# A decoder layer on one core: key-tile rotation on another engine, a third plain column block, a later split of the first down chunk

## The chip, the cores and the metric

One core of one Trainium2 chip runs the whole kernel. The metric is the device time of one execution in microseconds. Engines carry the profile's names: PE is TensorE (matmuls; PEld its weight loads), DVE is VectorE, ACT is ScalarE, POOL is GpSimd, SP is SyncE, which here only issues DMAs.

## What is computed

One layer of a decoder on 512 tokens of width 1024, all in float32, with three residual blocks:

```python
y = hybrid_mixer(rms_norm(x, pre_mix_g), w_in, attn_gn_g, ret_gn_g, w_out)
x = x + rms_norm(y, post_mix_g)
y = memory_cross_attn(rms_norm(x, pre_mem_g), mem, mem_norm_g, w_q_mem, w_kv_mem, w_o_mem)
x = x + rms_norm(y, post_mem_g)
y = (silu(g) * u) @ w_down          # g, u = split(rms_norm(x, pre_ffn_g) @ w_gate_up), hidden width 2816
x = x + rms_norm(y, post_ffn_g)
```

The mixer projects the input to queries, keys and values of 8 attention heads (64 wide) and of 4 retention heads (128 wide). Attention queries and keys get a rotary turn of their first 16 dimensions: `t * cos + swapped(t) * sin`. That turn of the keys is one place of the change; the SwiGLU at the end is the other.

## The kernel before

**Precision.** A float32 product is made of three passes of a faster type: every operand is split into a high part `h` (a cast, on ACT) and a low part `l` (the rest, a subtraction, on DVE; `split`, lines 90 and 91), and `mm3` (lines 84 to 86) adds up h*h, h*l and l*h in one PSUM bank. There are 8 PSUM banks of 128x512 (`bank`), 20 SBUF units of 128x2048 (`unit`, of which a split operand, `pair`, takes two), and 2 buffers for raw weights (`raw`).

**Order.** The program is traced in the order in which it is written. At build time the framework puts each engine's instructions in a fixed order, from the written order and its own estimate of when inputs are ready; a buffer goes to a new tile once the last reader of the old one is through. On the chip every engine works through its own queue in order. Inside `tc.manual_schedule()` (the loop over `step`) the written order is kept.

**Attention projections.** `head_proj` makes four tiles of two heads each for queries (`aq`) and then for keys (`ak`), f = 0 to 3: 24 matmuls of 128x512 each into one bank. Then DVE writes `t1 = ps * cos` (line 457) and `t2 = shuffle(ps)` (line 458); a multiply by sin (460) and an add (461) follow, on POOL for f = 0 to 2 and on DVE for f = 3. `flush` then splits the tile before: for keys `split_k` casts two halves on ACT (430), subtracts on DVE (432), copies on ACT (433), and moves the low half to the other 64 partitions by a DMA from POOL's queue (434). `att_scores` (lines 492 and 493) multiplies queries by these keys; its second matmul reads what that DMA wrote. Three banks hold one head's scores until DVE has masked them (497). The written order at the end of the keys is: ak 1, ak 2, scores of head 0, ak 3, scores of head 1, then the four value tiles `av`, each in one bank. At this time the last retention head is being normalised as well: its small DVE chain (186 to 190), its scaling on ACT (407) and its product with the gate on POOL (410).

**SwiGLU.** There are 22 column blocks of 128 gate and 128 up columns. A block is computed in one of two ways. `plain(f, j, n, ps)` is the direct product: for gate or up (j), for token half n, 24 matmuls of 128x256 (2 input halves, 4 chunks, 3 passes); a block has four such calls, 96 matmuls, and keeps two banks (`pg`). `step(f)` gets the same from seven block products in place of eight, 84 matmuls of 128x256, and needs sums of the weight blocks (`blocks_sum`), their split (`blocks_b`) and sums of the transposed input (T1 to T4). In a step, `ffn_c1` copies product 1 to `s1` (ACT, line 929), `ffn_c11` adds product 2 (DVE, 933), later adds read the other products (979, 981, 983, 984, 937). Product 7 goes into the bank that line 933 reads, product 3 into the one that line 979 reads.

Weights of a block come by one DMA into `raw` (`blocks_fetch`); `blocks_a` casts them on ACT (131), writes the negated cast (134), and a DMA from POOL's queue adds the weights onto that (135), which leaves the low part `wal`. For a plain block this is 2048 columns in pieces of 512, for a step 1536 in pieces of 768.

Two blocks (`PRE = 2`) are plain. They run while the last two token blocks of the layer before, `hb` and `hc`, are normalised and transposed (`to_b`, line 868, into B12 and B22 and the sums T): first both blocks for token half 0, then both for half 1. The operands of steps 2 and 3 are prepared in between. Then come steps 2 to 21. A step issues the loads, sums and splits of blocks after it, ahead of its own line 933. In the last step (f = 21) there is no block after it, and in that place stands `load()`, which splits the first chunk of the down weights (lines 90 and 91, two pieces).

**Down projection.** `down` multiplies the activations by `w_dn`: 11 chunks of 48 matmuls of 128x512, into all 8 banks. `split_a` reads the activations back from DRAM and splits them, the low part on POOL (1045).

Of the kernel before, what the change touches and what calls it, by code (L numbers as in the profile page):

```python
# [38 lines left out]
def hybrid_layer(ctx, tc, t, out):  # L39
    nc = tc.nc  # L40
# [9 lines left out]
    def uname(p):  # L50
        cnt[0] += 1
        return f"{p}{cnt[0]}"

    def bank(name):
        return psp.tile([P, 512], F32, tag="ps", name=uname(name))

    def unit(name, dt=F32):
        return up.tile([P, 2048], dt, tag="u", name=uname(name))

    def pair(name):  # L60
        return unit(name + "h", F32R), unit(name + "l", F32R)

    def work(name):
        return wk.tile([P, 512], F32, tag="w2k", name=uname(name))
# [14 lines left out]
    def part(pr, c0, n):  # L79
        return pr[0][:, c0:c0 + n], pr[1][:, c0:c0 + n]  # L80

    def mm3(o, sta, mov, start, stop):
        (sh, sl), (mh, ml) = sta, mov
        nc.tensor.matmul(o, lhsT=sh, rhs=mh, start=start, stop=False)  # L84
        nc.tensor.matmul(o, lhsT=sh, rhs=ml, start=False, stop=False)  # L85
        nc.tensor.matmul(o, lhsT=sl, rhs=mh, start=False, stop=stop)  # L86

    def split(src, hi, lo, scale=None):
        if scale is None:
            nc.scalar.copy(hi, src)  # L90
            nc.vector.tensor_sub(lo, src, hi.bitcast(F32))  # L91
        else:
            nc.scalar.mul(hi, src, scale)
            nc.vector.scalar_tensor_tensor(lo, src, scale, hi.bitcast(F32), op0=ALU.mult, op1=ALU.subtract)
# [6 lines left out]
    def fetch(key):  # L101
        fetched[key] = raw = rawp.tile([P, 2048], F32, tag="raw", name=uname("raw"))
        nc.sync.dma_start(raw, t[key[0]][key[1]])
# [6 lines left out]
    def blocks_fetch(f):  # L110
        chunks.remove(("w_gu", f))
        raws[f] = rawp.tile([P, 2048], F32, tag="raw", name=uname("raw"))
        nc.sync.dma_start(raws[f], t["w_gu"][f])

    def blocks_sum(f, names):
        if f not in sums:
            sums[f] = unit("sums")
        a11, a12, a22, a21 = (raws[f][:, i * 512:(i + 1) * 512] for i in range(4))
        s2, s4, s1, s3 = (sums[f][:, i * 512:(i + 1) * 512] for i in range(4))
        for name in names:  # L120
            e = nc.gpsimd if name in ('s3', 's4') else nc.vector
            if name == "s1":
                e.tensor_add(s1, a21, a22)
            else:
                e.tensor_sub(*{"s2": (s2, s1, a11), "s3": (s3, a11, a21), "s4": (s4, a12, s2)}[name])  # L125

    def blocks_a(f, n=1536, m=768):
        w = was[f] = pair("wa")
        for c0 in range(0, n, m):
            c = slice(c0, c0 + m)  # L130
            nc.scalar.copy(w[0][:, c], raws[f][:, c])  # L131
        for c0 in range(0, n, m):
            c = slice(c0, c0 + m)
            nc.scalar.mul(w[1][:, c], w[0][:, c].bitcast(F32), -1.0)  # L134
        nc.gpsimd.dma_start(w[1][:, :n], t["w_gu"][f][:, :n], accum_op=ALU.add)  # L135

    def blocks_b(f, i):
        if f not in wbs:
            wbs[f] = pair("wb")
        split(sums[f][:, i * 1024:(i + 1) * 1024], *part(wbs[f], i * 1024, 1024))  # L140
# [22 lines left out]
    def take(name, i, ahead=2):  # L163
        while (name, i) not in loaded:
            load()
        while chunks and len(loaded) - 1 < ahead:
            load()
        return loaded.pop((name, i))
# [61 lines left out]
    def hx(k, c0, n):  # L230
        return part(hT[k // 4], (k % 4) * S + c0, n)
# [209 lines left out]
    def flush():  # L441
        while late:
            fn, f, v = late.pop()
            fn(f, v)

    def head_proj(c0, store, name):
        ws = {}

        def one(f):
            if f % 2 == 0:  # L450
                ws[0] = take("w_in", c0 + f // 2)
            w = ws[0]
            ps = bank(name)
            for k in range(KT):
                mm3(ps, part(w, k * 256 + (f % 2) * P, P), hx(k, 0, S), k == 0, k == KT - 1)
            t1, t2 = work("t1"), work("t2")
            nc.vector.tensor_mul(t1, ps, rope[:, 2, :])
            nc.vector.stream_shuffle(t2, ps, swap)
            e = nc.vector if f == 3 else nc.gpsimd
            e.tensor_mul(t2, t2, rope[:, 3, :])  # L460
            e.tensor_add(t1, t1, t2)
            flush()
            late.append((store, f, t1))

        return [lambda f=f: one(f) for f in range(4)]
# [137 lines left out]
    ak = head_proj(10, split_k, "ak")  # L603
# [308 lines left out]
    def product(i, w, ps):  # L912
        u, c0, name = prods[i]
        for k in range(4):
            x_ = bx[name][:, k * H:(k + 1) * H], bx[name][:, 1024 + k * H:1024 + (k + 1) * H]
            mm3(ps, part(w[u], c0 + k * P, P), x_, k == 0, k == 3)
# [3 lines left out]
    def ffn_p12(f):  # L920

        w, p = (was[f], wbs[f]), bank("p")
        product(1, w, p[:, :H])
        product(2, w, p[:, H:])
        ffn[f] = w, p, work("s1"), work("c"), work("u")

    def ffn_c1(f):
        w, p, s1, c, u = ffn[f]
        nc.scalar.copy(s1[:, :H], p[:, :H])

    def ffn_c11(f):
        w, p, s1, c, u = ffn[f]
        nc.vector.tensor_add(c[:, :H], s1[:, :H], p[:, H:])

    def ffn_done(f):
        w, p, s1, c, u, r = ffn[f]
        nc.vector.tensor_add(c[:, H:], c[:, H:], r[:, H:])  # L937
        nc.scalar.activation(c, c, AF.Silu)  # L938

    def keep(f, v):  # L940
        nc.sync.dma_start(ad[:, f * S:(f + 1) * S], v)

    def ffn_mult(f):
        c, u = ffn.pop(f)[3:5]
        nc.vector.tensor_mul(c, c, u)
        keep(f, c)

    def step(f):
        nxt = f + 1 < FT
        two = f + 2 < FT  # L950
        ffn_p12(f)
        w, p, s1, c, u = ffn[f]
        if f + 3 < FT:
            blocks_fetch(f + 3)
        else:
            fetch(("w_dn", f + 3 - FT))
        if f > PRE:
            ffn_done(f - 1)
        if two:
            blocks_sum(f + 2, ("s3", "s1", "s2"))  # L960
        ffn_c1(f)
        if f > PRE:
            ffn_mult(f - 1)
        if nxt:
            blocks_b(f + 1, 1)
        else:
            load()
        ffn_c11(f)
        q, r = bank("q2"), bank("r")
        ffn[f] += (r,)  # L970
        product(4, w, q[:, :H])
        product(6, w, r[:, :H])
        if two:
            blocks_sum(f + 2, ("s4",))
        if nxt:
            blocks_b(f + 1, 0)
        if two:
            blocks_a(f + 2)
        nc.vector.tensor_add(s1[:, H:], s1[:, :H], r[:, :H])
        product(5, w, q[:, H:])  # L980
        nc.vector.tensor_add(c[:, H:], s1[:, H:], q[:, H:])
        product(7, w, p[:, :H])
        nc.vector.tensor_add(s1[:, :H], s1[:, H:], p[:, :H])
        nc.vector.tensor_add(u.rearrange("p (i s) -> p i s", i=2), q.rearrange("p (i s) -> p i s", i=2),
                             s1[:, None, :H].to_broadcast([P, 2, H]))
        product(3, w, r[:, H:])
        for d in (raws, was, sums, wbs):
            d.pop(f, None)


    PRE = 2

    def plain(f, j, n, ps):
        for i, (c0, name) in enumerate(((0, "B1%d"), (512, "B2%d")) if j == 0 else ((1536, "B1%d"), (1024, "B2%d"))):
# [4 lines left out]

    pg = {f: (bank("g"), bank("u")) for f in range(PRE)}  # L1000
    for f in range(PRE):
        blocks_fetch(f)
        blocks_a(f, 2048, 512)
    blocks_fetch(2)
    for f in range(PRE):
        for j in range(2):
            plain(f, j, 0, pg[f][j])
        if f == 0:
            late_splits = [to_b(hb, 2, nc.gpsimd)]
    late_splits.append(to_b(hc, 3))  # L1010
    blocks_a(2)
    blocks_sum(2, ("s3", "s1", "s2", "s4"))
    blocks_fetch(3)
    for f in range(PRE):
        for j in range(2):
            plain(f, j, 1, pg[f][j])
        if f == 0:
            for e in late_splits:
                e()
            late_splits.clear()  # L1020
        del was[f], raws[f]
        sg = work("sg")
        nc.scalar.activation(sg, pg[f][0], AF.Silu)
        nc.vector.tensor_mul(sg, sg, pg[f][1])
        keep(f, sg)
        blocks_b(2, 1 - f)
    pg.clear()
    del bx["B12"]
    blocks_a(3)
    blocks_sum(3, ("s3", "s1", "s2", "s4"))  # L1030
    blocks_fetch(4)
    xd = tc.dram_tile([S, D], F32, name="xd")
    for b in range(TB):
        nc.sync.dma_start(xd[b * P:(b + 1) * P, :], x[b])
# [150 lines left out]
```

## Time and profile before

| | |
|---|---|
| median of 3 runs | 802.81 us (799.59 to 955.97) |
| the profiled execution | 801.05 us |
| its span, first to last instruction | 799.3 us |
| outside the span | 1.75 us |
[...]
| busy, of the span | PE 98%, PEld 87%, DVE 63%, ACT 48%, POOL 25% |

Times in the rows are microseconds from the start of the span. A row of the timeline gives the start, the busy time, engine, line and operation, output and inputs, how many instructions are merged in it and, in brackets, how long the engine sat idle before it and who released it. PE's matmuls are pipelined: the busy time of one matmul overlaps the next one's, so that two matmuls of 256 columns start about 0.12 us apart while each is shown with 0.28 us, and two of 512 columns 0.23 us apart while each has 0.39.

### The profile page before, as it was taken

The page shows a single profiled execution, that of the slowest core. Times are in us where ns is not written, and L with a number is a line of the kernel's source. Part 1 is how long each engine was busy: PE and PEld are TensorE (multiplying, and loading weights), DVE is VectorE, ACT ScalarE, POOL GpSimd, SP SyncE. Part 2 cuts the span into 40 slices and gives each one's busy share as a digit, 9 for nine tenths or more (in the row PEclk, how much of TensorE's full clock was granted, in tenths as well). Part 3 has the DMA queues.
Part 4 walks back from the last instruction along what each step waited for, and adds up shares of the span by engine and source line. Part 5 has one row for each costly group of instructions (what it writes and reads, how often), then busy time and mean ns, then how long its engine had stood idle before and what let it go on. Part 6 is the DMA issues. An engine that isn't in the chain of part 4 may idle for free.

```text
span 799.3 us, 12220 instructions
## 1 busy us (share of the span) xinstructions
PE 780.2 (98%) x4828; PEld 695.8 (87%) x4828; DVE 502.5 (63%) x1002; ACT 386.4 (48%) x667; POOL 201.1 (25%) x177
## 2 busy tenths in 40 slices
PE   9999999899999999999999989999999999999996
PEld 7788888777887888999988989999999998888885
DVE  6497368574666657757567797667777767541143
ACT  6522424485563824445437575555555545542011
POOL 0163033420111100400000654333333326551000
PEclk9999999989999999999999999999999999999999
DMA  8634313223135430525008288777777793864011
GB/s 324 268 132 155 109 53 106 66 79 119 54 106 204 170 154 0 182 83 192 19 28 214 80 243 220 208 210 206 208 208 205 208 267 117 310 250 171 1 52 53
DMA packets 24489, 120.60 MB, mean 151 GB/s; under 512 B 2928, under 2 KB 2928, under 8 KB 14960
## 3 DMA queue, kind: packets, MB, share of 16 engines
q1 hardware_dynamic: 19904, 99.89, 34.3%
q0 software_dynamic: 3808, 18.88, 12.6%
q10 hardware_dynamic: 720, 1.06, 0.4%
q8 instruction: 38, 0.62, 0.3%
q14 instruction: 19, 0.16, 0.1%
HBM read 108.80 MB, written 9.96 MB: 149 GB/s over the span
## 4 chain that ended last, share of the span: by engine, by line
PE 52%; DVE 4%; issue 0%; ACT 0%; DVEq 0%; ACTq 0%
PE dn L84 5%; PE dn L85 5%; PE dn L86 5%; PE p L84 3%; PE p L86 3%; PE p L85 3%; PE q L85 3%; PE q L86 3%; PE q L84 3%; PE r L84 2%; PE r L86 2%; PE r L85 2%; PE o L84 2%; PE o L85 2%; PE o L86 2%; DVE wbl L91 1%
## 5 line engine op out<-in xcount | busy, mean ns | idle before, releaser
L91 DVE TENSOR_TENSOR wl<-raw,wh 128x1024 fp32r<-128x1024 f32 (+1 forms) x91 | 120.0, 1354 | 69.1 <-ACT wh L90 39.0
L90 ACT CAST wh<-raw 128x1024 fp32r<-128x1024 f32 (+1 forms) x91 | 90.0, 1038 | 61.4 <-DMA raw<-in_w_in 29.3
L91 DVE TENSOR_TENSOR wbl<-sums,wbh 128x1024 fp32r<-128x1024 f32 x40 | 51.2, 1280 | 30.3 <-ACT wbh L90 30.3
L84 PE MATMUL dn<-wh,ah 128*128 128x512 f32 x176 | 68.5, 389 | 0.0
L85 PE MATMUL dn<-wl,ah 128*128 128x512 f32 x176 | 68.5, 389 | 0.0
L86 PE MATMUL dn<-wh,al 128*128 128x512 f32 x176 | 68.5, 389 | 0.0
L135 POOL DMA_DIRECT2D wal<-in_w_gu x22 | 19.5, 887 | 176.1 <-ACT wal L134 117.5
L1045 POOL TENSOR_TENSOR al<-af,ah 128x512 fp32r<-128x512 f32 x22 | 36.1, 1673 | 43.9 <-ACT ah L1044 43.9
L84 PE MATMUL p<-bB,wah 128*128 128x256 f32 x160 | 45.3, 283 | 0.0
L85 PE MATMUL p<-bB,wah 128*128 128x256 f32 x160 | 45.3, 283 | 0.0
L86 PE MATMUL p<-bB,wal 128*128 128x256 f32 x160 | 45.3, 283 | 0.0
L90 ACT CAST wbh<-sums 128x1024 fp32r<-128x1024 f32 x40 | 40.2, 1051 | 3.4 <-POOL sums L125 1.8
L125 POOL TENSOR_TENSOR sums<-raw,sums 128x512 f32<-128x512 f32 x20 | 34.1, 1705 | 25.4 <-DVE sums L125 25.4
L86 PEld LDWEIGHTS dn<-wh,al 128*128 128x128 f32 x176 | 33.0, 188 | 6.9
L84 PEld LDWEIGHTS dn<-wh,ah 128*128 128x128 f32 x176 | 33.0, 188 | 6.8
L85 PEld LDWEIGHTS dn<-wl,ah 128*128 128x128 f32 x176 | 33.0, 188 | 6.8
L134 ACT ACTIVATE wal<-wah 128x768 fp32r<-128x768 f32 (+1 forms) x48 | 36.6, 809 | 0.0
L85 PE MATMUL q<-hhl,wh 128*128 128x256 f32 x128 | 36.2, 284 | 0.2 <-DVE hhl L91 0.2
L938 ACT ACTIVATE c<-c 128x512 f32<-128x512 f32 x20 | 12.7, 632 | 49.1 <-DVE c L937 49.1
L84 PE MATMUL q<-hhh,wh 128*128 128x256 f32 x128 | 35.8, 284 | 0.3 <-ACT hhh L90 0.3
L86 PE MATMUL q<-hhh,wl 128*128 128x256 f32 x128 | 36.1, 283 | 0.0
L131 ACT CAST wah<-raw 128x768 fp32r<-128x768 f32 (+1 forms) x48 | 35.9, 803 | 0.0
(346 smaller groups left out, 2521.5 us busy)
## 6 DMA issues: line engine op xcount, KB each, us to landing
raw<-in_w_gu SPq DMA_DIRECT2D x22, 1024.0 KB, 4.9
wal<-in_w_gu POOLq DMA_DIRECT2D x20, 768.0 KB, 7.3
raw<-in_w_in SPq DMA_DIRECT2D x12, 1024.0 KB, 5.0
raw<-in_w_dn SPq DMA_DIRECT2D x11, 1024.0 KB, 5.0
raw<-in_w_kv SPq DMA_DIRECT2D x8, 1024.0 KB, 4.7
ad<-c SPq DMA_DIRECT2D x20, 256.0 KB, 4.0
af<-ad SPq DMA_DIRECT2D x5, 1024.0 KB, 7.3
x<-in_x SPq DMA_DIRECT2D x4, 1024.0 KB, 9.5
```

The lines of the kernel that those rows point to most:

```text
L84: nc.tensor.matmul(o, lhsT=sh, rhs=mh, start=start, stop=False)
L85: nc.tensor.matmul(o, lhsT=sh, rhs=ml, start=False, stop=False)
L86: nc.tensor.matmul(o, lhsT=sl, rhs=mh, start=False, stop=stop)
L90: nc.scalar.copy(hi, src)
L91: nc.vector.tensor_sub(lo, src, hi.bitcast(F32))
L125: e.tensor_sub(*{"s2": (s2, s1, a11), "s3": (s3, a11, a21), "s4": (s4, a12, s2)}[name])
L131: nc.scalar.copy(w[0][:, c], raws[f][:, c])
L134: nc.scalar.mul(w[1][:, c], w[0][:, c].bitcast(F32), -1.0)
L135: nc.gpsimd.dma_start(w[1][:, :n], t["w_gu"][f][:, :n], accum_op=ALU.add)
L938: nc.scalar.activation(c, c, AF.Silu)
L1045: nc.gpsimd.tensor_sub(lo[:, c], v[:, c], hi[:, c].bitcast(F32))
```

## The change

The multiply and the add of the rotation go to DVE for all four key tiles; query tiles stay as they were. `PRE` becomes 3: block 2 is computed the plain way, and everything that was prepared for steps 2, 3 and fetched for 4 is now prepared for 3, 4 and fetched for 5. The two halves of `blocks_b` for the first step now follow the second and the third plain block. In the last step `load()` moves behind `ffn_c11`; for the other steps the order stays.

```diff
@@ head_proj
-            e = nc.vector if f == 3 else nc.gpsimd
+            e = nc.vector if f == 3 or name == 'ak' and f in (0, 1, 2) else nc.gpsimd
@@ step
         if nxt:
             blocks_b(f + 1, 1)
-        else:
+        ffn_c11(f)
+        if not nxt:
             load()
-        ffn_c11(f)
@@
-    PRE = 2
+    PRE = 3
@@
     for f in range(PRE):
         blocks_fetch(f)
         blocks_a(f, 2048, 512)
-    blocks_fetch(2)
+    blocks_fetch(PRE)
...
-    blocks_a(2)
-    blocks_sum(2, ("s3", "s1", "s2", "s4"))
-    blocks_fetch(3)
+    blocks_a(PRE)
+    blocks_sum(PRE, ("s3", "s1", "s2", "s4"))
+    blocks_fetch(PRE + 1)
...
-        blocks_b(2, 1 - f)
+        if f:
+            blocks_b(PRE, 2 - f)
...
-    blocks_a(3)
-    blocks_sum(3, ("s3", "s1", "s2", "s4"))
-    blocks_fetch(4)
+    blocks_a(PRE + 1)
+    blocks_sum(PRE + 1, ("s3", "s1", "s2", "s4"))
+    blocks_fetch(PRE + 2)
```

## Rows read from the trace of the kernel before

**Rows 1.** The page, part 1: busy time of each engine over the span.

```profile
PE 780.2 (98%) x4828; PEld 695.8 (87%) x4828; DVE 502.5 (63%) x1002; ACT 386.4 (48%) x667; POOL 201.1 (25%) x177
```

**Rows 2.** Waits of PE: who waited for whom, total, times, longest.

```profile
PE p L84 <- DVE c L933: 3.8, 2, 2.2
PE av L84 <- DVE t L458: 2.9, 1, 2.9
```

**Rows 3.** Busy time by stretch: PE, PEld, DVE, ACT, POOL, clock, DMA share, GB/s.

```profile
161.50:168.00 6.50, 6.45 (x16) 5.13 (x17) 4.64 (x15) 3.69 (x5) 3.64 (x4) 0.54 0.21 42
460.00:480.00 20.00, 17.24 (x140) 16.66 (x139) 19.64 (x24) 14.75 (x21) 10.93 (x8) 1.00 0.85 251
660.00:680.00 20.00, 18.33 (x123) 16.81 (x122) 14.01 (x16) 11.49 (x17) 12.52 (x8) 1.00 0.36 115
680.00:700.00 20.00, 20.00 (x90) 16.58 (x89) 10.30 (x6) 10.14 (x15) 11.14 (x6) 1.00 0.78 299
780.00:800.00 20.00, 12.10 (x54) 9.69 (x52) 7.43 (x21) 3.85 (x9) 0.00 (x0) 0.89 0.14 53
```

**Rows 4.** Timeline of PE around the key tiles.

```profile
150.59 0.47 PE L493 MATMUL s<-kl,qk 128*128 128x512 f32 x1 [1.46 <-DMA kl<-kl]
...
161.55 0.80 PE L84 MATMUL av<-wh,hTh 128*128 128x512 f32 x1 [2.92 <-DVE t L458]
```

**Rows 5.** Timeline of DVE around the key tiles.

```profile
152.67 0.73 DVE L458 STREAM_SHUFFLE t<-ak 128x512 f32<-128x512 f32 x1
158.72 1.41 DVE L432 TENSOR_TENSOR kl<-t,qk 64x512 fp32r<-64x512 f32 x2 [5.32 <-ACT qk L430]
...
160.77 0.72 DVE L458 STREAM_SHUFFLE t<-ak 128x512 f32<-128x512 f32 x1
...
168.25 0.69 DVE L460 TENSOR_TENSOR t<-t,rope 128x512 f32<-128x512 f32 x1
```

**Rows 6.** Timeline of POOL around the key tiles.

```profile
143.36 1.29 POOL L460 TENSOR_TENSOR t<-t,rope 128x512 f32<-128x512 f32 x1 [4.12 <-DVE t L458]
...
154.14 1.28 POOL L410 TENSOR_TENSOR rg<-rz,rg 128x512 f32<-128x512 f32 x1 [1.62 <-ACT rz L407]
...
156.75 1.29 POOL L461 TENSOR_TENSOR t<-t,t 128x512 f32<-128x512 f32 x1
```

**Rows 7.** DVE's rotation of the last query tile.

```profile
137.98 1.81 DVE L461 TENSOR_TENSOR t<-t,t 128x512 f32<-128x512 f32 x1
```

**Rows 8.** POOL's instruction at the same time.

```profile
137.94 1.29 POOL L410 TENSOR_TENSOR rg<-rz,rg 128x512 f32<-128x512 f32 x1 [1.62 <-ACT rz L407]
```

**Rows 9.** Timeline of PE: the first step (f = 2).

```profile
475.15 0.35 PE L84 MATMUL p<-bT,wbh 128*128 128x256 f32 x1 [2.16 <-DVE c L933]
...
477.29 0.39 PE L84 MATMUL r<-bB,wbh 128*128 128x256 f32 x1 [0.47 <-DVE s L979]
```

**Rows 10.** Timeline of DVE: line 933 in steps 3 and 4.

```profile
484.41 0.41 DVE L933 TENSOR_TENSOR c<-s,p 128x256 f32<-128x256 f32 x1
...
494.48 0.41 DVE L933 TENSOR_TENSOR c<-s,p 128x256 f32<-128x256 f32 x1
```

**Rows 11.** Timeline of ACT between the plain products.

```profile
439.94 0.60 ACT L687 ACTIVATE junk<-o 128x512 bf16<-128x512 f32 x1 [3.75 <-PE o L86]
...
444.94 1.06 ACT L196 ACTIVATE junk<-x 128x1024 bf16<-128x1024 f32 x1 [4.31 <-DVE x L699]
```

**Rows 12.** Timeline of PE: transposes of the last token block.

```profile
452.06 1.04 PE L868 MATMUL tp<-ident,h 128*128 128x128 f32 x8
```

**Rows 13.** Tile wal, 415 to 480 us: durations (min/median/max ns), and DMAs.

```profile
L134 ACT ACTIVATE wal<-wah x14: 636/680/850, 422.1 to 476.8; 128x512 fp32r<-128x512 f32 x8, 128x768 fp32r<-128x768 f32 x6
...
DMA to landing us min/median/max: 6.9/7.8/11.4
```

**Rows 14.** Timeline of DVE: the last step (f = 21).

```profile
664.70 4.12 DVE L91 TENSOR_TENSOR wl<-raw,wh 128x1024 fp32r<-128x1024 f32 x2 [0.36 <-ACT wh L90]
```

**Rows 15.** Timeline of PE: the last step.

```profile
669.29 0.35 PE L84 MATMUL p<-bT,wbh 128*128 128x256 f32 x1 [1.67 <-DVE c L933]
```

## The prediction

> **What bounds the kernel now.** I read the page's busy times first. PE is busy 98% of the span, 780.2 of 799.3 us [rows 1], and of the 19 us that it idles, 7 lie in the last stretch, where the final block leaves the chip [rows 3]. So nothing that only relieves another engine can pay, unless PE waits for that engine; and 2% of 802.81 us, 16 us, which is about what a measurement of this kernel can tell from no change, is more than all PE waits in the middle hold together. Next I read the waits of PE. The two largest are a product of the steps that waits for DVE's line 933, twice, 3.8 us, and the first value tile, which waits 2.9 us for DVE's shuffle [rows 2]. The windows show where these sit: in 460 to 480 PE is busy 17.24 of 20 us and DVE 19.64, in 660 to 680 PE 18.33 [rows 3]. [...] The change touches just these three places, so I price them one by one.
>
> A wait in brackets counts from the modelled end of the matmul before. Starts follow each other faster than these ends (0.23 apart at 0.39 us, 0.12 at 0.28), so PE's real loss is 0.16 us more than each idle shown.
>
> **Part 1, the key tiles.** What PE loses: 1.46 + 0.16 = 1.6 us before the second scores matmul, which waits for the DMA of the low key half [rows 4]; 2.92 + 0.16 = 3.1 us before the value tile [rows 4]; and 16 matmuls in 6.45 us where 16 x 0.23 = 3.7 would do, 2.7 us [rows 3]. Together 7.4 us, the upper bound.
>
> Why it waits: DVE shuffles a key tile, POOL takes 1.29 us each for multiply and add [rows 6], and only then may ACT cast and DVE subtract (line 432). DVE's queue is in order, so it stands idle in front of line 432, 5.32 us for key tile 1 [rows 5], and behind line 432 stands the shuffle of key tile 2. That shuffle is the last reader of the bank that the first value tile needs; all other banks hold scores or key tile 3. For tile 1 it was worse than two POOL operations: its shuffle was through at 153.4 [rows 5], POOL first did the gate product at 154.14, and its add ended at 156.75 + 1.29 = 158.0 [rows 6].
>
> With the change DVE itself does the two, 0.69 us each, as tile 3 shows [rows 5], with no hand-over. Six are added, 4.1 us of DVE; they lie in the 2 to 5 us that DVE idles per tile, so I charge them nothing as work, only as delay in the chain. If that cover were gone, 4.1 us of delay would be the price.
> - Tile 0: POOL started at 143.36 and took two times 1.29 [rows 6]; DVE needs 1.4. The DMA is issued 1.2 to 1.5 us earlier. The 1.6 us gap shrinks to about 0.2: gain 1.4 (bounds 0, if DVE first does its statistics for the retention head, and 1.6).
> - Tile 1: the chain ends at 153.4 + 1.4 = 154.8 in place of 158.0, 3.2 us earlier, and what stands ahead of it (a weight split behind tile 0's casts) also moves up by what tile 0 gains. Line 432 and the shuffle of tile 2 follow 3 to 4.6 us earlier. PE wants the bank 1.4 us earlier than its old 158.5. So of the 3.1 us gap 0 to 2.0 are left; I take 0.5: gain 2.6.
> - The clock: idles of 1.46 [rows 4] and 2.16 us [rows 9] left it at full speed (the stretch 460 to 480 shows 1.00 [rows 3]), the one of 2.92 us halved it. With 0.5 left I take the whole 2.7; the bound is 0.
>
> Sum of part 1: 1.4 + 2.6 + 2.7 = 6.7 us; from 1.1 (the gap stays at 2.0 and the clock still falls) to 7.4. POOL loses six operations of 1.29 us, and its only other work here is the key DMAs and the gate product, which come no later. Behind this stage PE stays full, so I take the gain as carried to the end: what feeds it (ACT's casts) was held by the same POOL chain.
>
> One row speaks against the move. DVE's add for the last query tile took 1.81 us [rows 7], where the same add takes 0.69; POOL's gate product ran beside it from 137.94 for 1.29 us [rows 8], and DVE was through 0.56 us behind POOL. [...] The moved pair of tile 1 would meet the gate product of 154.14. By this the gap keeps 1.1 us more (1.81 - 0.69) and the sum below would be 792.4, a time inside the forecast's own range, with some 0.2 of its chance.
>
> **Part 2, the third plain block.** It adds 96 matmuls of 128x256 and drops a step of 84. Lines 933 of two steps lie 494.48 - 484.41 = 10.07 us apart [rows 10], 0.12 us a matmul: 12 x 0.12 = 1.4 us more for PE, with nothing to hide it. A plain block is 96 x 0.12 = 11.5 us.
>
> What it takes away: in the first step PE loses 2.16 + 0.16 and 0.47 + 0.16 = 3.0 us [rows 9], both to DVE, which is full (19.64 of 20 us [rows 3]) with sums and splits that stand in its queue ahead of lines 933 and 979. With 11.5 us more of plain products in front of the first step, and only one more gate product (0.7 us) for DVE, that backlog (late by 2.3 us now) is done 11.5 - 0.7 - 2.3 = 8 us before it is needed. Gain 3.0, net 1.6. What is late next: steps 3 and on, where PE loses nothing.
>
> New in the preamble is the preparation of block 2: eight ACT operations of about 0.68 us [rows 13], 5.4 us, one DMA that lands up to 11.4 us after its issue [rows 13], two more units and two more PSUM banks. Before 440 all 20 units are taken, by my count of live tiles (residual 2, gains 1, w_o 8, cross-attention output 2, raw B 1, B11 and B21 2, two plain weight pairs 4). The first w_o chunk is free 18 matmuls before the output projection ends at 439.9 [rows 11], at 439.9 - 18 x 0.23 = 435.8. ACT idles 3.75 and 4.31 us on either side of 440 [rows 11], so the casts fit there, the DMA goes out at about 442 and lands at 450 to 453. PE reaches the point behind the second block at 452.06 [rows 12]. So the new block may cost PE 0 to 1 us there, and I take 0, as the scores and transposes of hc can go first. Banks: 6 for the plain blocks and 2 for each transposed pair make 8, the pair of hb being copied out before hc's. On SP's queue the fetch of block 4 now waits for the casts of block 2 instead of its sums: earlier, not later. Part 2 ranges from a gain of 2.0 (some short waits for hc's splits close too) to a loss of 7 (rivals).
>
> **Part 3, the last step.** Line 933 stood behind the two splits of the down chunk, 4.12 us from 664.70 [rows 14], and product 7 waited 1.67 + 0.16 = 1.8 us for it [rows 15]. Moved ahead, line 933 goes in the 0.36 us in which DVE waited for ACT's cast [rows 14], and the splits start where they did. Now line 979 is behind them, at 668.8, and ends at 669.2; product 7 then ends at 667.5 + 1.4 = 668.9, so product 3 loses 0.3. Gain 1.5. The splits end no later, so the first down matmul has its weights; the fetch for this chunk was issued two steps before, so no DMA moves.
>
> **The sum.** 6.7 + 1.6 + 1.5 = 9.8 us, made against the profiled execution's 801.05 us (span 799.3 and 1.75 outside it): **791.3 us**. That execution lies 1.8 us under the median, 802.81, and between the two lower runs.
>
> **Rivals.**
> - *Key chain still too slow* (chance 0.16). DVE no longer waits for POOL, but ACT's cast stands in ACT's queue behind the four retention scalings, or DVE's queue puts other work between. For it: every tile crosses DVE and ACT twice. Against: 3 us and more of margin were worked out. Part 1 gives 1.4 + 1.1 and the clock still falls: 801.05 - 2.5 - 1.6 - 1.5 = 795.4 us.
> - *Low part of block 2 late* (0.10). If its casts go only at 440.6, in ACT's second idle time, they end at 446, the DMA at 446.9 + 11.4 = 458.3. If PE's queue has block 2 next, it idles from 452.06, 6.2 us, and at half clock behind that 2.7. Part 2 becomes 6.2 + 2.7 + 1.4 - 3.0 = 7.3 us of loss: 801.05 - 6.7 - 1.5 + 7.3 = 800.2 us. For it: the units are full until 435.8. Against: PE has hc's transposes and half 1 of two blocks to do first.
> - *Slower* (0.07). The casts of block 2 get units that come free late. The residual is written until 444.94 [rows 11] and then copied out by a DMA, 6.9 us at the least by the nearest row [rows 13]: 452. If the casts stand in ACT's queue ahead of line 196 and wait for that unit, line 196 starts at 452 + 5.4 = 457.4 and all of hc is 12.5 us late; PE runs dry after two half blocks. It decides once the unit comes free later than 444.94. Part 2 is then 12.5 + 2.7 + 1.4 - 3.0 = 13.6 us of loss: 801.05 - 6.7 - 1.5 + 13.6 = 806.5 us. For it: 20 of 20 units taken. Against: ten units of the output projection come free first.
> - *Nothing gained* (0.07). The framework orders other instructions anew and gives the gain back: about 801 us. That the edits don't take effect can't be: the engine is named, and the loop keeps the written order.
>
> **How the numbers follow.** The forecast has 0.60. Its own range is 789.9 (all gaps closed: 7.4 + 2.0 + 1.8) to 794. A range of 787.5 to 800.5 takes in the first two rivals, and a run's scatter of some 2 us below. Only the sum of all gaps and some luck could pass 786.8 us: faster by over 2% gets 0.05. Slower by over 2% would be 818.9 us, past every case: 0.03. Within 2%: 0.92.
>
> **What would show it.** Part 1: the bracket at the first value tile under 1 us, the one before the second scores matmul near 0, clock 1.00 in 160 to 180, and no lines 460 and 461 on POOL for key tiles. Part 2: no wait of the first step (now f = 3) for lines 933 and 979, and PE full from 440 on; a gap at about 452 would be the late DMA. Part 3: product 7 of the last step without a wait, product 3 waiting about 0.3 for line 979. The prediction is wrong if PE still idles over 2 us at one place between 140 and 480 with the lower clock behind it, or if its first down matmul, at about 672 now, does not come some 10 us earlier.

## The result and the profile after

| | before | after |
|---|---|---|
| median of 4 runs each | 802.01 us (799.59 to 955.97) | 789.53 us (789.17 to 790.12) |
| the profiled execution | 801.05 us | 789.65 us |
| its span | 799.3 us | 787.9 us |
| granted TensorE clock over the span (1.00 is full speed) | 0.993 | 0.998 |

The ratio is 0.9855, 95% interval 0.9829 to 0.9881: 1.5% faster. The interval is a good deal narrower than the 2% that the prediction held to be about the least one can tell here. One slow execution of the kernel before, 955.97 us, counts in the median of the table and not in the ratio. Between the profiled executions 11.4 us are gone; 9.8 were forecast.

The page after, part 1, answers to [rows 1]: PE is now 99% of the span, with 12 matmuls more and 2.9 us less busy time. The stretch at a granted clock of 0.54 [rows 3], which is gone, had alone cost 2.7 us.

```profile
PE 777.3 (99%) x4840; PEld 694.5 (88%) x4840; DVE 498.3 (63%) x998; ACT 384.9 (49%) x668; POOL 189.1 (24%) x169
```

The waits of PE after, the three largest. Lines 933 and 458 of [rows 2] are gone from this list; of the wait for the key's DMA 0.4 us is left, and the two others stand ahead of 101 us, where nothing was edited.

```profile
PE warm L261 <- POOL ones L242: 1.0, 1, 1.0
PE bc L222 <- DVE diag L221: 0.6, 1, 0.6
PE s L493 <- DMA kl<-kl: 0.4, 1, 0.4
```

Busy time by stretch after, to set beside [rows 3] (columns as there). Where 16 matmuls ran at 0.54 there are 30 at 1.00; 460 to 480 and 660 to 680 are full.

```profile
161.50:168.00 6.50, 6.50 (x30) 5.37 (x30) 5.67 (x19) 6.49 (x21) 0.23 (x1) 1.00 0.20 40
...
460.00:480.00 20.00, 20.00 (x169) 20.00 (x168) 15.81 (x24) 13.29 (x18) 8.36 (x7) 1.00 0.81 244
...
660.00:680.00 20.00, 20.00 (x94) 16.70 (x93) 9.44 (x11) 10.43 (x14) 6.44 (x6) 1.00 0.81 312
```

The timeline of PE after: the second scores matmul and the first value tile [rows 4]; block 2's first matmul and first use of its low part `wal`; the transposes of `hc` [rows 12] and what follows; the first step, now f = 3 [rows 9]; products 7 and 3 of the last step [rows 15]; the first down matmul. A row without a bracket shows no idle before it.

```profile
149.37 0.47 PE L493 MATMUL s<-kl,qk 128*128 128x512 f32 x1 [0.35 <-DMA kl<-kl]
...
157.23 0.40 PE L84 MATMUL av<-wh,hTh 128*128 128x512 f32 x1
...
444.84 0.28 PE L84 MATMUL g<-bB,wah 128*128 128x256 f32 x1
...
445.08 0.28 PE L86 MATMUL g<-bB,wal 128*128 128x256 f32 x1
...
450.60 1.04 PE L868 MATMUL tp<-ident,h 128*128 128x128 f32 x8
451.88 0.39 PE L84 MATMUL g<-bB,wah 128*128 128x256 f32 x1 [0.24 <-ACT bB L885]
...
469.33 0.28 PE L84 MATMUL p<-bB,wah 128*128 128x256 f32 x1
...
657.97 0.28 PE L84 MATMUL p<-bT,wbh 128*128 128x256 f32 x1
...
659.41 0.28 PE L84 MATMUL r<-bB,wbh 128*128 128x256 f32 x1
...
660.85 0.40 PE L84 MATMUL dn<-wh,ah 128*128 128x512 f32 x1
```

Marks on PE (the start of the same matmul in two profiles) give the share of each part, as far as two single executions can. The first SwiGLU matmul comes at 432.47 where it came at 439.69: 7.2 us from part 1. Product 1 of step 3 comes at 469.33, not 478.82: 9.5, so part 2 adds 2.3. The first down matmul comes at 660.85, not 672.2: 11.4, so part 3 adds 1.9. Behind that nothing is won or lost.

The timeline of DVE after, around the keys [rows 5], at the first step [rows 10] and in the last [rows 14]:

```profile
151.82 0.73 DVE L458 STREAM_SHUFFLE t<-ak 128x512 f32<-128x512 f32 x1
152.59 0.69 DVE L460 TENSOR_TENSOR t<-t,rope 128x512 f32<-128x512 f32 x1
153.32 0.69 DVE L461 TENSOR_TENSOR t<-t,t 128x512 f32<-128x512 f32 x1
...
154.54 0.74 DVE L458 STREAM_SHUFFLE t<-ak 128x512 f32<-128x512 f32 x1
155.17 0.67 DVE L432 TENSOR_TENSOR kl<-t,qk 64x512 fp32r<-64x512 f32 x1
...
473.76 1.22 DVE L91 TENSOR_TENSOR wbl<-sums,wbh 128x1024 fp32r<-128x1024 f32 x1 [2.62 <-ACT wbh L90]
474.90 0.41 DVE L933 TENSOR_TENSOR c<-s,p 128x256 f32<-128x256 f32 x1
...
653.02 1.12 DVE L945 TENSOR_TENSOR c<-c,u 128x512 f32<-128x512 f32 x1 [1.63 <-ACT c L938]
654.25 0.42 DVE L933 TENSOR_TENSOR c<-s,p 128x256 f32<-128x256 f32 x1
655.20 3.46 DVE L91 TENSOR_TENSOR wl<-raw,wh 128x1024 fp32r<-128x1024 f32 x2 [0.53 <-ACT wh L90]
658.59 0.41 DVE L979 TENSOR_TENSOR s<-s,r 128x256 f32<-128x256 f32 x1
```

Two things are to be seen. At the first step DVE now waits for ACT (2.62 us) where it was late before. And at the keys the order itself is another: the shuffle of key tile 2 (154.54) stands ahead of line 432 of tile 1 (155.17), where in [rows 5] it stands behind it (158.72, then 160.77). The prediction did not see that coming, and the experiments on part 1 turn on it.

### The profile page after: what moved, and what is told of

Read it like the earlier page. It is cut to its first block, busy times and chain, and to the rows that moved or that the text cites. A ratio compares the mean times of both kernels' runs of the same rounds, so it can differ in the third digit from the quotient of the medians.

```text
span 787.9 us, 12232 instructions
## 1 busy us (share of the span) xinstructions
PE 777.3 (99%) x4840; PEld 694.5 (88%) x4840; DVE 498.3 (63%) x998; ACT 384.9 (49%) x668; POOL 189.1 (24%) x169
## 4 chain that ended last, share of the span: by engine, by line
PE 56%; DVE 1%; ACT 0%; issue 0%; DVEq 0%; ACTq 0%
PE dn L86 5%; PE dn L84 5%; PE dn L85 5%; PE p L85 3%; PE p L86 3%; PE p L84 3%; PE q L85 3%; PE q L86 3%; PE q L84 3%; PE r L85 2%; PE r L86 2%; PE r L84 2%; PE o L86 2%; PE o L84 2%; PE o L85 2%; PE g L84 1%
## 5 line engine op out<-in xcount | busy, mean ns | idle before, releaser
L91 DVE TENSOR_TENSOR wbl<-sums,wbh 128x1024 fp32r<-128x1024 f32 x38 | 46.6, 1229 | 30.5 <-ACT wbh L90 30.5
L85 PE MATMUL p<-bB,wah 128*128 128x256 f32 x152 | 43.1, 283 | 0.0
L84 PE MATMUL p<-bB,wah 128*128 128x256 f32 x152 | 43.0, 283 | 0.0
L86 PE MATMUL p<-bB,wal 128*128 128x256 f32 x152 | 43.0, 283 | 0.0
L90 ACT CAST wbh<-sums 128x1024 fp32r<-128x1024 f32 x38 | 38.0, 1051 | 0.0
L125 POOL TENSOR_TENSOR sums<-raw,sums 128x512 f32<-128x512 f32 x19 | 31.4, 1655 | 22.6 <-DVE sums L125 22.6
```

## The experiments

The gain of a run is given by its ratio to the kernel before on the same chip, and by PE's marks in its profile against the profile of before. The medians of before were 800.52 us (beside each part alone and parts 1 and 3), 799.48 (tile 0, tile 1, the gate product, the fourth plain block), 800.21 (the two hoists, the changed kernel once more) and 799.16 (the order alone).

### Each part alone

**Part 1 alone.**

```diff
-            e = nc.vector if f == 3 else nc.gpsimd
+            e = nc.vector if f == 3 or name == 'ak' and f in (0, 1, 2) else nc.gpsimd
```

> Part 1 alone: the key tiles' rotation on DVE, everything else as before. Theory (three separate PE gaps whose prices add): the first value matmul comes 4.3 us earlier and the stage after it is another 2.9 us ahead through the clock, 7.2 us in all, and that lead is carried to the last instruction: about 793.8 us against 801.0. Rival (the lead is given back where the two-part preparation of the steps is already late on DVE): PE arrives earlier at the first step but DVE's backlog there does not, so the wait for line 933 grows and less than 5 us is left: above 796 us.

Measured: 795.75 us, ratio 0.9941 (0.9922 to 0.9960), 2 us short of the theory's 793.8 and just below the rival's 796. The lead is 7.1 us at the first SwiGLU matmul and 6.5 at the first down matmul. No wait of PE grew in between, so the rival's reason does not hold. The 0.7 went in the first step: its wait is as long as before, but what follows it ran slower. PE's timeline and a stretch of 6 us from that matmul in this kernel:

```profile
468.01 0.36 PE L84 MATMUL p<-bT,wbh 128*128 128x256 f32 x1 [2.16 <-DVE c L933]
```

```profile
468.01:474.01 6.00, 6.00 (x37) 5.97 (x38) 4.79 (x8) 3.10 (x5) 2.84 (x3) 0.72 1.03 383
```

The same stretch of the kernel before, from its 475.15 [rows 9]:

```profile
475.15:481.15 6.00, 5.53 (x44) 5.33 (x45) 5.61 (x8) 3.10 (x5) 2.88 (x3) 1.00 0.99 369
```

An idle of 2.16 us, followed by clock 1.00 and 44 matmuls in one and by 0.72 and 37 in the other: 7 x 0.12 = 0.8 us. Nothing in the step was edited; the idle only lies 7 us earlier. That leads from the theory's 793.8 to what this execution took, 794.57; the median lies another 1.2 above it.

**Part 2 alone.** The changed kernel without the other two edits.

```diff
-            e = nc.vector if f == 3 or name == 'ak' and f in (0, 1, 2) else nc.gpsimd
+            e = nc.vector if f == 3 else nc.gpsimd
...
-        ffn_c11(f)
-        if not nxt:
+        else:
             load()
+        ffn_c11(f)
```

> Part 2 alone: the third plain block, rotation and last step as before. Theory: the key-tile gaps stay (3 us idle, then the lower clock), the first step shows no wait for lines 933 and 979, net gain 2.3 us: about 798.7 us. Rival (the new block's preparation only fitted because part 1 had moved things): the low part of block 2 is late, PE idles behind the second block, no gain or a loss: 801 us or more.

Measured: 798.02 us, ratio 0.9964 (0.9949 to 0.9980), near the theory's 798.7; PE does not idle behind the second block. The first step has no wait; the value tile waits 2.90 us as before, and the last step 1.13 us for line 933. But behind that 2.90 us the loss was smaller than in [rows 3]: 21 matmuls in 6.5 us, clock 0.74, in the stretch of this kernel:

```profile
161.50:168.00 6.50, 6.42 (x21) 5.18 (x22) 4.64 (x16) 3.65 (x5) 3.65 (x4) 0.74 0.21 42
```

That is 6.4 - 21 x 0.23 = 1.6 us lost, not 2.7. The next kernel's profile shows 0.74 after 2.92 us as well.

**Part 3 alone.**

```diff
-        else:
-            load()
         ffn_c11(f)
+        if not nxt:
+            load()
```

> Part 3 alone: in the last step the split of the first down chunk behind line 933. Theory: product 7 of the last step starts without a wait, the first down matmul 1.5 to 1.9 us earlier, about 799.3 us. Rival (the down projection is bound by its weights or by POOL's low parts): the lead shrinks to under 0.5 us by the end: 800.6 us or more.

Measured: 798.17 us, ratio 0.9976 (0.9961 to 0.9991), 1.1 us below the theory's 799.3. In the last step product 7 does not wait. Product 3 does, 0.25 us, close to the 0.3 of the forecast (PE of this kernel):

```profile
667.74 0.38 PE L84 MATMUL r<-bB,wbh 128*128 128x256 f32 x1 [0.25 <-DVE s L979]
```

Its first down matmul comes at 669.28, 2.9 us ahead of the profile of before. Of that, 1.6 us stand already at the first SwiGLU matmul (438.13 against 439.69), ahead of anything edited: so far do two profiles of the same code differ. Counted from product 1 of step 3, part 3 is worth 1.4 us here.

The three ratios add up to -1.19%, 9.5 us of 800; all three together gave more, by the middle of the intervals, so the next kernel leaves out one.

**Parts 1 and 3**, without the third plain block.

```diff
-            e = nc.vector if f == 3 else nc.gpsimd
+            e = nc.vector if f == 3 or name == 'ak' and f in (0, 1, 2) else nc.gpsimd
...
-        else:
-            load()
         ffn_c11(f)
+        if not nxt:
+            load()
```

> Parts 1 and 3 without part 2 (two plain blocks). Theory (prices add): 801.0 - 7.2 - 1.9 = 791.9 us, the first step again shows about 2.9 us of waits for lines 933 and 979. Rival (part 2 carries more than its own gap): 793 us or more.

Measured: 793.17 us, ratio 0.9914 (0.9889 to 0.9940): the rival's number. The first step waits 2.15 us again, and again at clock 0.72 behind it. Its first down matmul is at 664.2, that of the changed kernel at 660.85: on top of the other two parts the plain block is worth 3.4 us, of which 0.8 is this clock.

### Part 1: the engine, or the order?

**Only key tile 0 on DVE**, tiles 1 and 2 stay on POOL.

```diff
-            e = nc.vector if f == 3 else nc.gpsimd
+            e = nc.vector if f == 3 or name == 'ak' and f in (0,) else nc.gpsimd
```

> Only key tile 0 rotates on DVE, else the kernel before. Theory (each tile's POOL chain holds the queue of DVE by itself): the wait before the second scores matmul falls from 1.46 to about 0.4 us, a gain of about 1.2 us there; the wait at the first value tile stays at some 3 us with the lower clock behind it: about 799.8 us, and if the idle grows to 4 us no gain at all. Rival (the chain of tile 0 sets the later ones): the second wait goes too, 794 us.

Measured: 793.87 us, ratio 0.9941 (0.9926 to 0.9955), the rival's number, and the same ratio as all three tiles. The value tile doesn't wait, though tile 1's rotation is still POOL's. DVE of this kernel shows why:

```profile
151.33 0.74 DVE L458 STREAM_SHUFFLE t<-ak 128x512 f32<-128x512 f32 x1
...
152.56 0.75 DVE L458 STREAM_SHUFFLE t<-ak 128x512 f32<-128x512 f32 x1
156.63 2.81 DVE L432 TENSOR_TENSOR kl<-t,qk 64x512 fp32r<-64x512 f32 x2 [3.33 <-ACT qk L430]
```

DVE still idles 3.33 us in front of line 432, but the shuffle that frees the value tile's bank is already done. The framework's build-time order had changed. So the theory that each tile's own chain must be shortened falls.

**Only key tile 1 on DVE.**

```diff
-            e = nc.vector if f == 3 else nc.gpsimd
+            e = nc.vector if f == 3 or name == 'ak' and f in (1,) else nc.gpsimd
```

> Only key tile 1 rotates on DVE, else the kernel before. Theory: the first wait stays at 1.46 us; the 2.92 us wait at the first value tile falls to under 0.5 us and with it the stretch at the lower clock: gain 3.1 + 2.7 = 5.8, about 795.2 us. Rival (tile 2's own POOL work is needed too, or the six moved operations act together): the wait stays above 1.5 us, 797 us or more.

Measured: 796.27 us, ratio 0.9965 (0.9949 to 0.9981). Here the order stayed as in [rows 5]. The wait before the second scores matmul is 1.52 us, as before; the value tile waits 0.85 us, and the clock stays at 1.00 behind it. Time and wait lie between the theory's (795.2 and under 0.5) and the rival's (797 and above 1.5). DVE, POOL and PE of this kernel:

```profile
153.75 1.80 DVE L461 TENSOR_TENSOR t<-t,t 128x512 f32<-128x512 f32 x1
156.24 1.41 DVE L432 TENSOR_TENSOR kl<-t,qk 64x512 fp32r<-64x512 f32 x2 [0.69 <-ACT qk L430]
...
158.29 0.72 DVE L458 STREAM_SHUFFLE t<-ak 128x512 f32<-128x512 f32 x1
```

```profile
153.72 1.29 POOL L410 TENSOR_TENSOR rg<-rz,rg 128x512 f32<-128x512 f32 x1 [1.62 <-ACT rz L407]
```

```profile
159.07 0.50 PE L84 MATMUL av<-wh,hTh 128*128 128x512 f32 x1 [0.85 <-DVE t L458]
```

This is the case that the prediction had worked out, a faster chain in the old order, with DVE's add beside POOL's gate product, which began 0.03 us before it: the add took 1.80 us for 0.69.

**The order alone**: all rotations stay on POOL, and key tile 2 keeps its written order, in which its shuffle stands ahead of tile 1's split.

```diff
-    rest[1]()
+    with tc.manual_schedule():
+        rest[1]()
```

> The kernel before, with all key rotations left on POOL; only the written order is kept for key tile 2 (a second manual_schedule around it). In DVE's queue this puts lines 457 and 458 of tile 2 ahead of line 432 of tile 1, in POOL's queue the two rotation operations of tile 2 ahead of tile 1's two key DMAs. Theory (the order is what the gap before the value tile hangs on, not the engine of the rotation): tile 2's shuffle comes right behind tile 1's, at about 154, so the value tile does not wait (2.92 + 0.16 us) and the clock stays up behind it (2.7 us); the wait before the second scores matmul, 1.46 us, stays. Gain 5.8 us: 800.2 - 5.8 = 794.4 us by the medians, and every mark behind the value tiles 5.8 earlier. Rival (the time POOL takes for tile 1 is what holds everything): ACT's cast and line 432 still come at 158.7, scores and later tiles follow them, and the value tile waits as before or another wait of 2 to 3 us stands a little later: 798 to 800.5 us.

Measured: 795.46 us, ratio 0.9957 (0.9942 to 0.9972); the theory had 794.4, the rival 798 or more. DVE and PE of this kernel:

```profile
152.08 0.73 DVE L458 STREAM_SHUFFLE t<-ak 128x512 f32<-128x512 f32 x1
...
153.31 0.73 DVE L458 STREAM_SHUFFLE t<-ak 128x512 f32<-128x512 f32 x1
158.13 1.12 DVE L432 TENSOR_TENSOR kl<-t,qk 64x512 fp32r<-64x512 f32 x1 [4.09 <-ACT qk L430]
```

```profile
157.90 0.40 PE L84 MATMUL av<-wh,hTh 128*128 128x512 f32 x1
```

With no work moved to another engine the value tile's wait is gone, and the first SwiGLU matmul comes at 434.07, 5.6 us earlier than in the profile of before (5.8 expected). By medians the gain is 3.7 us, by the ratio 3.4 (2.2 to 4.6). The yardstick makes most of this difference: three other profiles with the value tile's wait (parts 2 and 3 alone, the gate product) reach that matmul at 438.1 to 438.7, and against them the order gains 4.1 to 4.6. PE also waits 0.8 us at 280 now, for splits of the output projection's weights. DVE's line 432 comes about as late as before. So with the chain as slow as ever the order alone removes the wait; a faster chain in the old order, as with tile 1, shortens it as well.

**The other occupant of POOL**: the gate product of the last retention head on DVE, keys on POOL.

```diff
-        nc.gpsimd.tensor_mul(rgh, z.rearrange("p (b d) -> p b d", b=TB), rgh)
+        (nc.vector if h == 3 else nc.gpsimd).tensor_mul(rgh, z.rearrange("p (b d) -> p b d", b=TB), rgh)
```

> The rotation stays on POOL as before; the gate product of the last retention head, which stood in front of key tile 1's rotation in POOL's queue, goes to DVE. Theory (the length of the chain through POOL is what PE waits for, the gate product is 2.0 us of its 4.6): tile 1's rotation starts at about 153.5 in place of 155.4, the wait at the first value tile falls from 2.9 to about 1 us, the clock stays at full speed: gain about 4.6 us, 796.4 us. Rival A (any POOL rotation is too slow): the wait stays above 2.5 us, about 800.5 us. Rival B (the gate product in POOL's queue was the whole cause): the wait goes to 0, 795 us.

Measured: 799.89 us, ratio 1.0009 (0.9994 to 1.0025): nothing, where a gain was expected. It is rival A's number, but not its test, since another thing moved too. DVE of this kernel:

```profile
154.05 0.69 DVE L410 TENSOR_TENSOR rg<-rz,rg 128x512 f32<-128x512 f32 x1 [1.34 <-ACT rz L407]
...
154.67 0.73 DVE L458 STREAM_SHUFFLE t<-ak 128x512 f32<-128x512 f32 x1
```

The framework put the product ahead of tile 1's shuffle. DVE waits there for ACT's scaling, the shuffle comes 2.0 us later than in [rows 5], so that POOL's rotation starts no earlier than before, and the value tile waits 3.04 us.

### Part 2: what the first step waits for

**One line hoisted.** Parts 1 and 3, and in the first step line 933 goes ahead of the splits of the next block. Against the kernel of parts 1 and 3:

```diff
+        if f == PRE:
+            ffn_c11(f)
         if nxt:
             blocks_b(f + 1, 1)
-        ffn_c11(f)
+        if f != PRE:
+            ffn_c11(f)
```

> Parts 1 and 3, two plain blocks, and in the first step line 933 is issued ahead of the first half of the next step's weight split. Theory (the gap of the first step is DVE's backlog as a whole, and line 979 stands behind the same splits): product 7 no longer waits, but product 3 then waits for line 979 until about the same instant, so nothing or at most 0.3 us is gained on the kernel with parts 1 and 3 alone: about 791.9 us. Rival (line 933 by itself is what holds PE): 2.3 us gained, 789.6 us.

Measured: 793.90 us, ratio 0.9927 (0.9913 to 0.9940), nothing over the two parts. Product 7 is free, and product 3 waits in its place; product 7 of the next step then waits 0.78 us (PE of this kernel; its line 982 is the old 979):

```profile
470.23 0.39 PE L84 MATMUL r<-bB,wbh 128*128 128x256 f32 x1 [2.75 <-DVE s L982]
...
479.90 0.35 PE L84 MATMUL p<-bT,wbh 128*128 128x256 f32 x1 [0.78 <-DVE c L933]
```

**Both lines hoisted**: also line 979 goes ahead of both split calls (the main lines against parts 1 and 3).

```diff
-        if nxt:
+        if f == PRE:
+            ffn_c11(f)
+        elif nxt:
             blocks_b(f + 1, 1)
...
+        if f == PRE:
+            nc.vector.tensor_add(s1[:, H:], s1[:, :H], r[:, :H])
+            blocks_b(f + 1, 1)
```

> As the one with line 933 ahead, but products 4 and 6 and line 979 of the first step also stand ahead of both halves of the next step's weight split. Theory (what PE waits for is only the place of two short DVE instructions behind long ones; the splits themselves are needed 3 us later): both waits go without the 1.4 us of a third plain block: about 3 us under the kernel with parts 1 and 3, 789.0 us, 0.5 under the changed kernel. Rival (the backlog is real work that then holds up the second step): a wait of 1 to 3 us shows in the step after, 790.5 us or more.

Measured: 792.41 us (790.45 to 796.64), ratio 0.9916 (0.9891 to 0.9940), slower than the changed kernel, 789.63 on the same chip. In the profile the first step is free of waits. The second waits 3.75 us, since DVE stood idle for weights that came late, and behind this wait the clock is 0.53: 29 matmuls in 6 us, some 2.4 us more lost (DVE, PE and a stretch of this kernel):

```profile
474.41 0.69 DVE L123 TENSOR_TENSOR sums<-raw 128x512 f32<-128x512 f32 x1 [2.75 <-DMA raw<-in_w_gu]
```

```profile
480.09 0.55 PE L84 MATMUL p<-bT,wbh 128*128 128x256 f32 x1 [3.75 <-DVE c L933]
```

```profile
480.00:486.00 6.00, 5.91 (x29) 5.94 (x30) 4.10 (x7) 0.00 (x0) 0.73 (x1) 0.53 0.96 244
```

This execution took 796.07 us, at a mean clock of 0.993. It and one other (796.64) are the two slowest of six; the four others took 790.45 to 792.59 at 0.997 to 0.999, and whether they wait in the second step is not shown. So one hoist shows that the wait is handed on, and two hoists show that a late fetch can take its place (2.75 of the 3.75 us). At its best the kernel with both (790.45) comes within 0.8 us of the changed kernel's median, but it scatters far more. DVE's backlog in the first step is work that an order moves elsewhere; the 11.5 us of a third plain block in front of it leave DVE idle there (2.62 us, above).

**A fourth plain block** on top of the change.

```diff
-    PRE = 3
+    PRE = 4
...
+        if f == 3:
+            pg[f] = bank("g"), bank("u")
...
+            for n in (0, 1) if f == 3 else (1,):
+                plain(f, j, n, pg[f][j])
...
```

> All of the change, and a fourth plain block (block 3, both token halves behind the other three). Theory (with three blocks no gap is left to close, so one more costs its 12 matmuls): 1.4 us slower than the changed kernel, about 790.9 us, no new wait at the first step. Rival (the longer lead still hides something, or the preparation of block 3 leaves PE dry): 789 us, or 793 us and more with a new PE gap before the first step.

Measured: 791.11 us, ratio 0.9905 (0.9889 to 0.9922). No wait is left to close, none is new, and from the first SwiGLU matmul to the first down matmul it is 229.8 us, where the changed kernel takes 228.4. The 1.4 us are the price of the 12 matmuls by itself, as forecast.

### The changed kernel once more

No edit: the changed kernel, on the same chip as the two hoists.

> The changed kernel itself, beside the two above on one chip, as their yardstick. All theories: 789.5 us.

Measured: 789.63 us (789.52 to 791.80), ratio 0.9871 (0.9854 to 0.9888). The 791.80 is the profiled execution, and it shows a wait that the other profile lacks. PE and ACT of it (line 1045 here is the cast of `split_a`, 1044 in the kernel before):

```profile
661.43 0.39 PE L84 MATMUL r<-bB,wbh 128*128 128x256 f32 x1 [1.64 <-DVE s L979]
```

```profile
652.70 2.18 ACT L1045 CAST ah<-af 128x512 fp32r<-128x512 f32 x4 [6.44 <-DMA af<-ad]
654.79 0.63 ACT L938 ACTIVATE c<-c 128x512 f32<-128x512 f32 x1
```

ACT waits for activations read back for the down projection; in the first profile it is through with that wait 2.4 us earlier. Line 938 stands behind it in ACT's queue, DVE's line 945 waits for 938, and lines 933, the down splits and 979 follow. Then product 3 waits 1.64 us for line 979, where the first profile shows 0 and part 3 alone 0.25.

## Why the prediction was right

**The forecast.** 791.3 us was 1.8 above the median of 789.53, inside the range, and the waits that it named went, but for 0.35 us at the scores. Between the two profiles the terms are 7.2, 2.3 and 1.9 us against 6.7, 1.6 and 1.5 forecast. But the profile of before flatters the first. Three other profiles with the gap at the value tile (parts 2 and 3 alone, the gate product) reach the first SwiGLU matmul at 438.1 to 438.7, not 439.69; against them part 1 gains 5.7 to 6.2 us. Part 1 alone gained 4.7 by its ratio (3.2 to 6.2), after the clock in the first step had taken back some 0.8. So part 1 was forecast somewhat too large and the two others too small, and that the sum came so close is partly luck.

**Part 1, near the size, wrong reason in one step.** The terms between the two profiles: 1.46 - 0.35 = 1.1 at the scores (1.4 forecast), the whole 3.1 at the value tile (2.6), and the clock, 2.7. The step that failed reads "Line 432 and the shuffle of tile 2 follow 3 to 4.6 us earlier". Line 432 did come 3.5 us earlier, but the shuffle came 6.2 us earlier, because it no longer follows line 432. With the old order the step holds: tile 1 alone on DVE brought both 2.5 us forward, 3.6 without the 1.1 by which DVE's add took longer beside POOL's product (1.80 for 0.69), and left 0.85 us of the gap. The order alone, on POOL, closes that gap as well. Moving tiles 1 and 2 added nothing measurable over tile 0. Part 1's gain is thus the earlier tile 0 at the scores, and a changed order at the value tile. All rotations on DVE with the old order held was not run. As an estimate, tile 1's rest of 0.85 us is less than those 1.1, so the faster chain might have closed the gap too; in the changed kernel it did not have to. "The framework orders other instructions anew" stood in the forecast only as a way to lose. What makes the framework's estimate tip over with tile 0 stays open.

**The clock term was a single execution's.** The 2.7 us of [rows 3] are right for that profile. Three others of kernels with this gap (2.90, 2.92 and 3.04 us) show 0.74 and 21 matmuls in 6.5 us from the idle's end, so 1.6 us or a little more. That goes with a gain of 11.4 us between the two profiles, and of 10.6 between the medians on the chip of the last yardstick (800.21 and 789.63). That idles of 1.46 and 2.16 us left the clock at full speed (1.00 over the 6 us behind each, in the profile of before) did not hold for other kernels: after 2.14 to 2.16 us in the first step the clock is 0.72 in three profiles (part 1, tile 0, parts 1 and 3) and 1.00 in five (before, part 3, tile 1, the gate product, the order alone).

**DVE beside POOL.** In the changed kernel DVE's lines 460 and 461 kept their 0.69 us, and POOL's gate product, which began 0.19 us behind line 461, took longer; its row after, to set beside [rows 6] with 1.28:

```profile
153.51 1.66 POOL L410 TENSOR_TENSOR rg<-rz,rg 128x512 f32<-128x512 f32 x1 [1.62 <-ACT rz L407]
```

With tile 1 alone POOL began 0.03 us ahead and DVE's add took 1.80, as in the kernel before, where POOL began 0.04 ahead and the add took 1.81 [rows 7, 8]. In all three the one that began later took longer, and ended 0.54 and 0.56 (DVE) and 1.16 us (POOL) behind the other, a little under its own length of 0.69 and 1.28. What holds it back the traces do not show. The prediction charged DVE with 1.1 us; which engine pays hung on starts 0.03 to 0.19 us apart.

**Part 2, right; a margin misread.** The gap of 3.0 closed, the 12 matmuls cost the 1.4 (the fourth block), and some shorter waits without a bracket closed as well (at 470.10 in the kernel before two starts lie 0.41 us apart where 0.12 is due): net 2.3, the forecast's upper bound being 2.0. On top of part 1 it also saves the 0.8 us of clock in the first step. But the reason given against "low part of block 2 late", that PE has hc's transposes first, was wrong. PE's queue has block 2 at 444.84, ahead of the transposes at 450.60. What kept it free of a wait is that the units came free earlier than my count said. ACT's casts after:

```profile
425.21 2.22 ACT L131 CAST wah<-raw 128x512 fp32r<-128x512 f32 x4
```

On the old time scale that is 432.4, where the first unit was expected at 435.8. POOL's DMA for the low part went out at 431.49, and it landed later than any of [rows 13]; the tile's landing time after:

```profile
DMA to landing us min/median/max: 13.1/13.1/13.1
```

431.49 + 13.1 = 444.6, and its first reader is the matmul of 445.08: 0.5 us of margin. So the reason given against that rival did not hold, and the wait was missed by half a microsecond.

**Part 3, right.** Product 7's 1.8 us went. The 0.3 charged to product 3 was 0 in one profile, 0.25 in part 3 alone and 1.64 in another: the term was too firm, for it hangs on a DMA at the far end of ACT's and DVE's queues. With the 0.25 part 3 alone is worth 1.4 us, with 0 the 1.9 of the changed kernel.

**Where the sum of the parts falls short.** Alone they give 9.5 us, together 10.6 on the chip of the yardstick. The intervals of the three ratios, some 1.5 us each, are too wide to call the 1.1 a difference. The profiles show one cause that works this way: the clock in the first step, 0.8 us, which part 1 alone loses, and part 2 takes that idle away.

**What stays open.** Why the same idle lowers the clock in one kernel and not in another. In the three profiles with 0.72 the idle ended at 467.4 to 468.1 us of the span, in the five with 1.00 at 469.5 to 475.2; no run varied that moment, or PE's work ahead of the idle, alone.

## What to carry to other kernels

When PE waits for a short instruction of another engine, look first at what stands ahead of it in that engine's queue: here another order alone was worth 3.4 us, and moving six instructions to DVE (0.69 us each for POOL's 1.29), which changed the order too, 4.7, with intervals that overlap. Moving two instructions of an earlier tile, or one product, was enough to change that order at build time, for better or for worse. Price an idle's clock loss from several profiles, as a range that starts at zero. Here time in front of it closed the wait for an engine that was behind with its work; hoisting the one line waited for only handed the wait on.

## What the hardware showed that was not expected

- After an idle of 2.15 us the granted clock over the next 6 us was 1.00 or 0.72, after 2.75 us 1.00 in the kernel with one line hoisted, after 2.9 to 3.0 us 0.54 or 0.74 over 6.5 us, and after 3.75 us 0.53 in the kernel with both. The length of the idle alone does not tell.
- Times of the kernel before follow the granted clock. Of 58 executions beside the experiments the eight at a mean of 0.997 took 797.3 to 798.4 us, the four at 0.991 801.5 to 802.6. The profile of before, at 0.993, lost 2.7 us behind the value tile's idle; the three with the same idle at 0.995 and 0.996 lost 1.6. Without such idles eight executions of the changed kernel took 789.17 to 790.12, but for one of 791.80, and four with a fourth plain block 790.99 to 791.38.
- The 1 MB DMAs that add weights onto the negated cast took 11.4 and 11.3 us to land in the kernel before, which has two of them, and 11.9, 11.8 and 13.1 us in the changed kernel, which has three, issued at 418.99, 425.67 and 431.49. The last is beyond all of [rows 13].
